# A decoder layer on one core: order of the first loads, order of the products in a chunk, transposes of the identity at the start, rotation tables earlier

## Chip, cores and metric

The kernel runs on one core of one Trainium2 chip. The metric is device time in microseconds (us) of one execution. The median of three runs is given, and one more execution was profiled.

## The reference, cut to what matters

One layer for 256 tokens of 2048 features, in float32: a gated feed-forward half (FFN), a mixer of retention and sliding-window attention side by side, a second FFN half, and a gated embedding, each followed by a layer norm. What the change touches is the first FFN and the cosine and sine tables of the rotary positions.

```python
def swiglu(x, w_gu, w_down):
    g, u = jnp.split(x @ w_gu, 2, axis=-1)
    return (jax.nn.silu(g) * u) @ w_down
...
def rotary(x, pos, n_rot, theta):
    half = n_rot // 2
    inv = 1.0 / (theta ** (jnp.arange(half, dtype=jnp.float32) / half))
    ang = pos.astype(jnp.float32)[..., None] * inv
    cos = jnp.cos(ang)[:, :, None, :]
    sin = jnp.sin(ang)[:, :, None, :]
...
h = layer_norm(alpha * h + 0.5 * swiglu(h, w_ffn1_gu[i], w_ffn1_down[i]), ln_g[i, 0], ln_b[i, 0])
```

## The kernel before

**Products.** A float32 product is made of three passes over a high and a low part of each operand. `split` (L91, L92) makes the parts: ScalarE casts the high part, then VectorE subtracts it to get the low part. `Sum.add` issues the three matmuls of 128x512 (L298: low left part by high right part, L299: high by high, L300: high by low). The weights come as chunks of 512 KB: `Chunk` loads one (L105), and `make` splits it. In the trace a gate or up chunk is rf_gu when raw, and hf_gu and lf_gu are its parts. A chunk holds two tiles of 128 features (k tiles). The 256 tokens are two halves t = 0 and 1, each with a PSUM bank of its own. `tokens_chunk` walks over halves and k tiles, so a chunk that serves both halves is 12 matmuls.

**Blocks.** The gate and up products of the first FFN go in 11 blocks (`ffn`, `block`), tiles f1g and f1u. Block 0 has eight ordinary units, each a gate chunk and an up chunk over the same two k tiles: 16 chunks. Later blocks have ordinary units and some of seven products (`Seven`): VectorE forms the sums u and v of a pair of chunks (L163 to L166), and these and the raw chunks are split (huf_gu, luf_gu, hvf_gu, lvf_gu, bf_gu among the results). Their extra sums go to the banks f11s in block 1 and f12s in block 2. They need sums of the inputs, which `seven_forms` makes ahead of unit 7 of block 0 (tiles sums, f1fh, f1fl). At the end of block 0, ScalarE applies Silu to the gate banks (L833) and VectorE multiplies by the up banks (L835), giving f1v. Two takes of chunks later, `turned` transposes the result on TensorE against the identity (f1t, L774), and ScalarE copies it out of its banks (f1a, L776).

**Order of the work.** Each engine runs its instructions in the order in which the program wrote them (`manual_schedule`). `plan` is the list of weight units in their order of use. `fill` is called after each unit and writes two kinds of work. It writes the split of the next loaded unit while the units that are ready are worth under 45 matmuls and while the slots allow it. It writes loads of further units, if after the load there is still room to split the unit in front. `slots_for_weights` sets how many slots weights may use, 6 at the start and 24 from unit 6 of block 0. A raw ordinary chunk needs one slot and a split one keeps two. So 6 slots hold the splits one chunk ahead of the products. Slots are counted as the program is written, not as it runs. Loads go on SyncE's DMA queue, the first chunk and the constants on that of ScalarE. A transfer's completion semaphore is one of eight in turn, so a queue waits until the transfer eight places earlier in the program has landed.

**The start.** `first_chunk` and `load_x_chunk` bring in x, transposed, in four parts (xraw, split into xt). A part has four k tiles, and the first one comes as four pieces of 128 KB. The first weight chunk comes as two halves on ScalarE's queue. ident, the identity for transposes, is written by GpSimd at the start. At unit 2 of block 0 `load_constants` issues four small transfers on ScalarE's queue, and `rotary_tables` is appended to `lazy`. It is a generator. Each `next` writes one step: the load of the positions; their cast (L689) with six operations on the angle (L696 to L701); pairs of L704; a last L704; a clamp (L708); a sine on ScalarE (L710); five operations (L712 to L716); a cosine (L718). The steps from the angle on come twice, for retention (rotr) and for attention (rota). `run_side`, called after each chunk, runs one such step.

Of the kernel before, what the change touches and what calls it, by code (L numbers as in the profile page):

```python
# [15 lines left out]
P = 128  # L16
S = 256
# [11 lines left out]

HELD_MIX = 4  # L30
FRONT = 6
FRONT_PAIRS = 3
HELD_PAIRS = 2, 3
SLOTS = 46
# [14 lines left out]
def layer(ctx: ExitStack, tc: tile.TileContext, io):  # L49
    nc = tc.nc  # L50
    sync, act, dve, pool, pe = nc.sync, nc.scalar, nc.vector, nc.gpsimd, nc.tensor
# [8 lines left out]
    def bank(name):  # L60
        return psum.tile([P, 512], F32, tag="ps", name=name)
# [12 lines left out]
    plan = []  # L74
# [15 lines left out]
    def split(dst_hi, dst_lo, src, lo_engine=None):  # L90
        act.copy(dst_hi, src)  # L91
        (lo_engine or dve).tensor_tensor(dst_lo, src, dst_hi, ALU.subtract)  # L92
# [88 lines left out]
    loaded, ready = [], []  # L181
    room = {"slots": 0, "used": 0, "ahead": 45, "far": 90, "quiet": False}
# [41 lines left out]
    def slots_for_weights(n, ahead=45, far=90):  # L224
        room.update(slots=n, ahead=ahead, far=far)
# [5 lines left out]
    lazy = []  # L231
# [71 lines left out]
        return tuple(x[:, t * P : (t + 1) * P] for x in a)  # L303

    def tokens_chunk(chunk, k0, lhs, sums, ts, kks=(0, 1)):
        for t in ts:
            for kk in kks:
                sums[t].add(half_of(lhs(k0 + kk), t), chunk.columns(kk))

    def tokens_out(key, n_k, lhs, ps, n=512, before=None):  # L310
# [352 lines left out]
    ident = const.tile([P, P], F32, name="ident")  # L663
# [7 lines left out]
    ht = big.tile([P, KD, 512], F32R, tag="ht", name="xt")  # L671
# [12 lines left out]
    def rotary_tables():  # L684
        pos_i = slot([P, S], I32, "pos_i")
        act.dma_start(pos_i, io["positions"].broadcast_to([P, S]))
        pos = slot([P, S], F32, "pos")
        yield
        dve.tensor_copy(pos, pos_i)  # L689
        table = slot([P, 4, S], F32, "trig")  # L690
        trig.extend(table[:, j, :] for j in range(4))
        cos_r, sin_r, cos_a, sin_a = trig
        for inv, sgn, cos, sin, nm in ((0, 2, cos_r, sin_r, "r"), (1, 3, cos_a, sin_a, "a")):
            w = slot([P, 4, S], F32, "rot" + nm)
            ang, n, na, nb = (w[:, j, :] for j in range(4))
            dve.tensor_scalar(ang, pos, cst[:, inv : inv + 1], None, ALU.mult)  # L696
            dve.tensor_scalar(n, ang, INV_2PI, MAGIC, ALU.mult, ALU.add)
            dve.tensor_scalar(n, n, MAGIC, None, ALU.subtract)
            dve.tensor_scalar(na, n, 1.0 / 2048.0, MAGIC, ALU.mult, ALU.add)
            dve.tensor_scalar(na, na, MAGIC, 2048.0, ALU.subtract, ALU.mult)  # L700
            dve.tensor_tensor(nb, n, na, ALU.subtract)  # L701
            yield
            for who, j in ((na, 0), (nb, 0), (na, 1), (nb, 1), (na, 2), (nb, 2), (na, 3)):
                dve.scalar_tensor_tensor(ang, who, -TWO_PI[j], ang, ALU.mult, ALU.add)  # L704
                if who is nb:
                    yield
            yield
            dve.tensor_scalar(n, ang, 3.1415925, -3.1415925, ALU.min, ALU.max)  # L708
            yield
            act.activation(nb, n, AF.Sin)  # L710
            yield
            dve.tensor_scalar(sin, nb, cst[:, sgn : sgn + 1], None, ALU.mult)  # L712
            dve.tensor_scalar(na, ang, 1.5707963267948966, None, ALU.add)
            dve.tensor_scalar(n, na, 3.141592653589793, -6.283185307179586, ALU.is_gt, ALU.mult)
            dve.tensor_tensor(na, na, n, ALU.add)
            dve.tensor_scalar(na, na, 3.1415925, -3.1415925, ALU.min, ALU.max)  # L716
            yield
            act.activation(cos, na, AF.Sin)  # L718
            yield
# [35 lines left out]

    def ffn(name, i, ht, norm, keep, residual, keepers, away):
        if i == 0:
            slots_for_weights(6)
        rhs = lambda k: (ht[:, k, :S], ht[:, k, S:])
        raws = []  # L760
        made = {}
# [23 lines left out]
        for j in range(KF // 4):  # L785
            pg, pu = banks(f"{name}g{j}"), banks(f"{name}u{j}")
            units = gu_units(j)
            plain = len(units) - sum(kind == "S" for kind, p in units)
            n_of = {(0, 0): KD, (0, 1): KD, (1, 0): KD, (1, 1): KD}
            for kind, p in units:  # L790
                if kind == "S":
                    for at in ((0, 0), (0, 1), (1, 0)):
                        n_of[at] -= 1
                    n_of[1, 1] -= 2
            sums = [[Sum((pg, pu)[n][t], n_of[t, n]) for n in range(2)] for t in range(2)]
            got = []

            if norm is not None and j == 0:
                front, units = units[:FRONT_PAIRS], units[FRONT_PAIRS:]
                steps = [(gu_keys(name, 0)(n, p), 2 * p, n) for _, p in front for n in range(2)]  # L800
                norm.first(steps, rhs, sums, (
                    (3, (1, 0)), (5, (1, 1)), (7, (0, 2)), (8, (1, 2)), (9, (0, 3)), (10, (1, 3)), (10, "go"),
                ))
                slots_for_weights(24)

            def before(u, j=j, offset=KD // 2 - len(units)):
                u += offset
                if j == 0 and norm is None and u % 2 == 0:
                    first_chunk(u // 2)
                    if u == 6:  # L810
                        slots_for_weights(24)
                    if u == 2:
                        load_constants()
                        lazy.append(rotary_tables())
                if j == 0 and u == 7:
                    for g in sorted({p // 2 for p in SEVEN}):
                        hi, lo = (slot([P, 8, P], F32R, f"{name}f{w}{g}") for w in "hl")
                        made[g] = seven_forms(keep[g], hi, lo)
                if j == KF // 4 - 1 and u in (4, 6):
                    convert(u // 2 - 2)  # L820

            block(f"{name}{j}", units, gu_keys(name, j), rhs, forms, sums, lambda *a: got.extend(seven_common(*a)), before)
            if got:
                g, v = got
                for x, ps in ((g, pg), (v, pu)):
                    for t in range(2):
                        dve.tensor_tensor(x[:, t], x[:, t], ps[t], ALU.add)  # L827
                act.activation(g, g, AF.Silu)  # L828
                dve.tensor_tensor(v, g, v, ALU.mult)
            else:  # L830
                v = slot([P, 2, 512], F32, f"{name}v{j}")
                for t in range(2):
                    act.activation(v[:, t], pg[t], AF.Silu)  # L833
                for t in range(2):
                    dve.tensor_tensor(v[:, t], v[:, t], pu[t], ALU.mult)  # L835
            later(2, lambda j=j, v=v: turned(j, v))
# [558 lines left out]
    x_parts = {}  # L1395

    def load_x_chunk(c):
        raw = slot([P, 4, S], F32, f"xraw{c}")
        x_parts[c] = raw
        pieces = 4 if c == 0 else 1  # L1400
        parts = [slice(j * 4 // pieces, (j + 1) * 4 // pieces) for j in range(pieces)]
        for at in parts:
            sync.dma_start(raw[:, at], io["xT"][c][:, at])
        if c == 0:
            u = plan.pop(0)
            u.load(pieces=2, queue=act)
            u.chunk.make_hi()
            room["used"] += u.keeps
            ready.append(u)
        for j, at in enumerate(parts):  # L1410
            to = ht[:, 4 * c : 4 * c + 4, :][:, at]
            split(to[:, :, :S], to[:, :, S:], raw[:, at])
            if c == 0 and j < 2:
                u.chunk.make_part(u.chunk.parts[j])

    with tc.manual_schedule():
        warm = small.tile([P, 1], F32, tag="nc1", name="warm")
        dve.memset(warm, 0.0)
        act.activation(warm, warm, AF.Silu)
        plan_ffn("f1")  # L1420
        plan.extend(Single(("w_pp", blk, 0)) for blk in range(2))
        plan_mixers()
        plan.extend(Single(("w_pp", blk, 0)) for blk in range(2, 4))
        plan_ffn("f2")
        for blk in range(4):
            plan_tokens(("w_pg", blk), KD)
        kept = sorted({p // 2 for p in SEVEN})
        norm = ffn("f1", 0, ht, None, x_parts, x_columns, (), rows[0])
        norm = mixers(norm.new, norm, rows[0], kept, rows[1])
        norm = ffn("f2", 2, norm.new, norm, norm.keep, rows[1], (), None)  # L1430
        embedding(norm.new, norm, norm.y)
        assert not (plan or loaded or ready or side or lazy) and not room["used"]
# [100 lines left out]
```

## Time and profile before

| | |
|---|---|
| three runs | 2291.86, 2292.39, 2293.10 us |
| profiled execution | 2292.7 us, span 2290.8 us |
| mean granted TensorE clock | 0.998 |
| TensorE busy | 2266.2 us |
| VectorE busy | 1945.5 us |
| ScalarE busy | 1183.6 us |
| HBM read, written | 455.43 MB, 8.39 MB |

In the profile PE is TensorE, PEld its loading of stationary operands, DVE VectorE, ACT ScalarE, POOL GpSimd and SP SyncE. A q behind a name means the queue or sequencer of that engine. The timeline gives start, duration, engine, line, operation and tiles (out<-in). In brackets stands the idle time of the engine before the instruction, with what ended it. In the list of waits a line gives who waited for whom, then the total in us, how many times, and the longest. In the windows each engine has its busy time and in brackets its number of instructions, in the order PE, PEld, DVE, ACT, POOL, followed by the clock, the DMA share and GB/s. All times are from the start of the span.

### The profile page before, as it was taken

Reading aid. Unit: us, or ns where it says so; the run is one execution under the profiler, and the core shown is the slowest. Engines: PE = TensorE matmul, PEld = TensorE weight load, DVE = VectorE, ACT = ScalarE, POOL = GpSimd, SP = SyncE. Lnnn points to the kernel's source line nnn. Section 1 sums busy time; section 2 is a strip of 40 time slices with the busy share of each in tenths; the row PEclk is TensorE's granted clock in tenths of the full one; section 3 lists DMA queues with packets and bytes.
Section 4 is the critical chain, followed back from the end, with each engine's and each line's share of the span. In section 5 each row is a group of like instructions: output and inputs, shape, how many; then the busy total and the mean of one; then the engine's idle time right before and its main releaser. Section 6 shows DMA issues by size and latency. Waiting matters only on the chain.

```text
span 2290.8 us, 28764 instructions
## 1 busy us (share of the span) xinstructions
PE 2266.2 (99%) x10466; PEld 1879.6 (82%) x10466; DVE 1945.5 (85%) x2467; ACT 1183.6 (52%) x1427; POOL 95.8 (4%) x53
## 2 busy tenths in 40 slices
PE   9999999999999999999999999999999999999997
PEld 7788888888888888888778888888888888888876
DVE  7999999998989774677789786779999999889876
ACT  5555555555554342435556454355565555555532
POOL 0000000000000530124000000000000000000000
PEclk9999999999999999999999999999999999999999
DMA  9576666665587565555447567576656566565771
GB/s 317 167 220 193 185 210 197 190 203 191 209 287 275 181 227 163 171 165 158 138 156 238 168 223 276 186 234 208 194 190 211 183 199 216 182 221 193 276 275 55
DMA packets 193725, 465.70 MB, mean 203 GB/s; under 512 B 14768, under 2 KB 16048, under 8 KB 193584
## 3 DMA queue, kind: packets, MB, share of 16 engines
q1 hardware_dynamic: 191456, 460.91, 60.9%
q10 hardware_dynamic: 2128, 2.97, 0.4%
q8 instruction: 82, 1.34, 0.2%
q14 instruction: 59, 0.48, 0.1%
HBM read 455.43 MB, written 8.39 MB: 202 GB/s over the span
## 4 chain that ended last, share of the span: by engine, by line
PE 96%; DVE 3%; DMA 1%; issue 0%; ACT 0%; SPq 0%; ACTq 0%; DVEq 0%
PE f1g L298 3%; PE f1g L299 3%; PE f1g L300 3%; PE f2g L298 3%; PE f2g L300 3%; PE f2g L299 3%; PE rqk L249 3%; PE f1u L299 2%; PE f1u L300 2%; PE f1u L298 2%; PE f2u L298 2%; PE f2u L299 2%; PE f2u L300 2%; PE aqk L249 2%; PE f1d L300 2%; PE f2d L299 2%
## 5 line engine op out<-in xcount | busy, mean ns | idle before, releaser
L92 DVE TENSOR_TENSOR lf_gu<-rf_gu,hf_gu 128x1024 fp32r<-128x1024 f32 (+1 forms) x283 | 334.5, 1215 | 10.2 <-ACT hf_gu L91 9.8
L91 ACT CAST hf_gu<-rf_gu 128x1024 fp32r<-128x1024 f32 (+1 forms) x283 | 281.9, 1046 | 18.5 <-DMA rf_gu<-in_f_gu 18.5
L92 DVE TENSOR_TENSOR lw_in_f<-rw_in_f,hw_in_f 128x1024 fp32r<-128x1024 f32 x140 | 195.7, 1428 | 29.2 <-ACT hw_in_f L91 26.6
L92 DVE TENSOR_TENSOR lf_down<-rf_down,hf_down 128x1024 fp32r<-128x1024 f32 x152 | 181.0, 1221 | 27.9 <-ACT hf_down L91 23.5
L91 ACT CAST hf_down<-rf_down 128x1024 fp32r<-128x1024 f32 x152 | 155.2, 1050 | 76.0 <-DMA rf_down<-in_f_down 26.4
L91 ACT CAST huf_gu<-uf_gu 128x1024 fp32r<-128x1024 f32 x70 | 73.7, 1054 | 159.4 <-DVE uf_gu L164 156.8
L91 ACT CAST hw_in_f<-rw_in_f 128x1024 fp32r<-128x1024 f32 x140 | 138.9, 1051 | 2.4 <-DMA rw_in_f<-in_w_in_f 2.1
L298 PE MATMUL f1g<-hf_gu,xt 128*128 128x512 f32 x247 | 97.2, 393 | 5.4 <-ACT hf_gu L91 5.4
L299 PE MATMUL f1g<-hf_gu,xt 128*128 128x512 f32 x247 | 96.8, 392 | 0.0
L300 PE MATMUL f1g<-lf_gu,xt 128*128 128x512 f32 x247 | 96.8, 392 | 0.0
L298 PE MATMUL f2g<-hf_gu,ht 128*128 128x512 f32 x247 | 96.3, 390 | 0.0
L300 PE MATMUL f2g<-lf_gu,ht 128*128 128x512 f32 x247 | 96.2, 389 | 0.0
L299 PE MATMUL f2g<-hf_gu,ht 128*128 128x512 f32 x247 | 96.1, 389 | 0.0
L91 ACT CAST hvf_gu<-vf_gu 128x1024 fp32r<-128x1024 f32 x70 | 73.8, 1054 | 29.5 <-DVE vf_gu L166 28.9
L828 ACT ACTIVATE eve<-eve 128x1024 f32<-128x1024 f32 x20 | 21.2, 1062 | 127.0 <-DVE eve L827 127.0
L92 DVE TENSOR_TENSOR luf_gu<-uf_gu,huf_gu 128x1024 fp32r<-128x1024 f32 x70 | 85.3, 1219 | 0.0
L92 DVE TENSOR_TENSOR lvf_gu<-vf_gu,hvf_gu 128x1024 fp32r<-128x1024 f32 x70 | 85.3, 1218 | 0.0
L298 PE MATMUL f2u<-hf_gu,ht 128*128 128x512 f32 x212 | 83.7, 395 | 0.0
L298 PE MATMUL f1u<-hf_gu,xt 128*128 128x512 f32 x212 | 83.4, 393 | 0.0
L300 PE MATMUL f2u<-lf_gu,ht 128*128 128x512 f32 x212 | 82.6, 390 | 0.0
L299 PE MATMUL f2u<-hf_gu,ht 128*128 128x512 f32 x212 | 82.6, 389 | 0.0
L299 PE MATMUL f1u<-hf_gu,xt 128*128 128x512 f32 x212 | 82.5, 389 | 0.0
(1333 smaller groups left out, 6425.9 us busy)
## 6 DMA issues: line engine op xcount, KB each, us to landing
rf_gu<-in_f_gu SPq DMA_DIRECT2D x351, 512.0 KB, 4.9
rf_down<-in_f_down SPq DMA_DIRECT2D x176, 512.0 KB, 4.5
rw_in_f<-in_w_in_f SPq DMA_DIRECT2D x148, 512.0 KB, 4.3
rw_rv<-in_w_rv SPq DMA_DIRECT2D x32, 512.0 KB, 4.7
rw_ret<-in_w_ret SPq DMA_DIRECT2D x32, 512.0 KB, 4.5
rw_mix<-in_w_mix SPq DMA_DIRECT2D x32, 512.0 KB, 3.9
rw_pg<-in_w_pg SPq DMA_DIRECT2D x32, 512.0 KB, 5.2
rw_att<-in_w_att SPq DMA_DIRECT2D x16, 512.0 KB, 4.9
```

Source lines behind the costliest of these rows:

```text
L91: act.copy(dst_hi, src)
L92: (lo_engine or dve).tensor_tensor(dst_lo, src, dst_hi, ALU.subtract)
L249: pe.matmul(ps[f], hi[:, kk, f * P : (f + 1) * P], rhs(k), start=k == 0, stop=k == n_k - 1,)
L298: pe.matmul(o, al, bh, start=first, stop=False)
L299: pe.matmul(o, ah, bh, start=False, stop=False)
L300: pe.matmul(o, ah, bl, start=False, stop=self.left == 0)
L828: act.activation(g, g, AF.Silu)
```

## The change

The first part of x comes as three pieces (one k tile, one k tile, two k tiles). The second weight chunk is loaded ahead of the third piece. Nine slots instead of six are open to weights until unit 6 of block 0. `tokens_chunk` takes k tile by k tile, both halves of the tokens for each, instead of half by half. Fourteen transposes of the identity stand on TensorE ahead of the first product. The generator of the rotation tables gets one more step ahead of each of the units 4 to 7 of block 0.

```diff
@@ -29,6 +29,8 @@
 
 HELD_MIX = 4
 FRONT = 6
+
+WARM = 14
 FRONT_PAIRS = 3
 HELD_PAIRS = 2, 3
 SLOTS = 46
@@ -303,8 +305,8 @@
         return tuple(x[:, t * P : (t + 1) * P] for x in a)
 
     def tokens_chunk(chunk, k0, lhs, sums, ts, kks=(0, 1)):
-        for t in ts:
-            for kk in kks:
+        for kk in kks:
+            for t in ts:
                 sums[t].add(half_of(lhs(k0 + kk), t), chunk.columns(kk))
 
     def tokens_out(key, n_k, lhs, ps, n=512, before=None):
@@ -755,7 +757,7 @@
 
     def ffn(name, i, ht, norm, keep, residual, keepers, away):
         if i == 0:
-            slots_for_weights(6)
+            slots_for_weights(9)
         rhs = lambda k: (ht[:, k, :S], ht[:, k, S:])
         raws = []
         made = {}
@@ -812,6 +814,8 @@
                     if u == 2:
                         load_constants()
                         lazy.append(rotary_tables())
+                if j == 0 and u >= 4 and lazy and next(lazy[0], "end") == "end":
+                    lazy.pop(0)
                 if j == 0 and u == 7:
                     for g in sorted({p // 2 for p in SEVEN}):
                         hi, lo = (slot([P, 8, P], F32R, f"{name}f{w}{g}") for w in "hl")
@@ -1397,21 +1401,36 @@
     def load_x_chunk(c):
         raw = slot([P, 4, S], F32, f"xraw{c}")
         x_parts[c] = raw
-        pieces = 4 if c == 0 else 1
-        parts = [slice(j * 4 // pieces, (j + 1) * 4 // pieces) for j in range(pieces)]
-        for at in parts:
+        if c:
+            sync.dma_start(raw, io["xT"][c])
+            split_x(c, slice(0, 4))
+            return
+        parts = [slice(0, 1), slice(1, 2), slice(2, 4)]
+        for at in parts[:2]:
             sync.dma_start(raw[:, at], io["xT"][c][:, at])
-        if c == 0:
-            u = plan.pop(0)
-            u.load(pieces=2, queue=act)
-            u.chunk.make_hi()
-            room["used"] += u.keeps
-            ready.append(u)
+        u = plan.pop(0)
+        u.load(pieces=2, queue=act)
+        u.chunk.make_hi()
+        room["used"] += u.keeps
+        ready.append(u)
+        plan[0].load()
+        room["used"] += plan[0].loads
+        loaded.append(plan.pop(0))
+        sync.dma_start(raw[:, parts[2]], io["xT"][c][:, parts[2]])
         for j, at in enumerate(parts):
-            to = ht[:, 4 * c : 4 * c + 4, :][:, at]
-            split(to[:, :, :S], to[:, :, S:], raw[:, at])
-            if c == 0 and j < 2:
+            split_x(c, at)
+            if j < 2:
                 u.chunk.make_part(u.chunk.parts[j])
+
+    def split_x(c, at):
+        to = ht[:, 4 * c : 4 * c + 4, :][:, at]
+        split(to[:, :, :S], to[:, :, S:], x_parts[c][:, at])
+
+    def warm_up():
+
+        ps = bank("warm")
+        for _ in range(WARM):
+            pe.transpose(ps[:, :P], ident, ident)
 
     with tc.manual_schedule():
         warm = small.tile([P, 1], F32, tag="nc1", name="warm")
@@ -1425,6 +1444,7 @@
         for blk in range(4):
             plan_tokens(("w_pg", blk), KD)
         kept = sorted({p // 2 for p in SEVEN})
+        warm_up()
         norm = ffn("f1", 0, ht, None, x_parts, x_columns, (), rows[0])
         norm = mixers(norm.new, norm, rows[0], kept, rows[1])
         norm = ffn("f2", 2, norm.new, norm, norm.keep, rows[1], (), None)
```

## The prediction

> **What bounds the kernel now.** I read the page first, then TensorE's waits in the first 130 us, then the timelines of TensorE, ScalarE, VectorE and the DMA queue there, because the change acts there and nowhere else by design. TensorE's waits after 113 us were listed too: 3.3 us in all, every one at a norm.
>
> ```profile
> PE 2266.2 (99%) x10466; PEld 1879.6 (82%) x10466; DVE 1945.5 (85%) x2467; ACT 1183.6 (52%) x1427; POOL 95.8 (4%) x53
> PE 96%; DVE 3%; DMA 1%; issue 0%; ACT 0%; SPq 0%; ACTq 0%; DVEq 0%
> ```
>
> TensorE is busy for 99% of the span and carries 96% of the chain that ended last. The change takes no product away, so it can only win back waits or slow matmuls. The waits of the first 130 us:
>
> ```profile
> PE f1g L298 <- ACT hf_gu L91: 5.4, 2, 5.2
> PE f12s L298 <- ACT f1a L776: 1.0, 1, 1.0
> PE f11s L300 <- DVE luf_gu L92: 0.6, 1, 0.6
> PE f11s L300 <- DVE lvf_gu L92: 0.2, 1, 0.2
> ```
>
> 5.2 us pass before the first product, 0.2 us at the second half chunk, and 1.8 us in blocks 1 and 2. Slow matmuls show in TensorE's timeline:
>
> ```profile
> 8.94 0.63 PE L299 MATMUL f1g<-hf_gu,xt 128*128 128x512 f32 x1
> 9.37 0.57 PE L300 MATMUL f1g<-lf_gu,xt 128*128 128x512 f32 x1
> 9.78 0.39 PE L298 MATMUL f1g<-hf_gu,xt 128*128 128x512 f32 x1
> 10.01 0.40 PE L299 MATMUL f1g<-hf_gu,xt 128*128 128x512 f32 x1
> ```
>
> Starts are 0.43 us apart until 9.8 us and 0.227 us apart after it (0.227 is the median from 10 us on). All that is slow is some ten matmuls: 10 x 0.20 = 2.0 us. Now the supply of the first two chunks and of the positions, on ScalarE and VectorE:
>
> ```profile
> 6.39 0.62 ACT L91 CAST hf_gu<-rf_gu 128x512 fp32r<-128x512 f32 x1 [0.90 <-DMA rf_gu<-in_f_gu]
> 8.47 1.04 ACT L91 CAST hf_gu<-rf_gu 128x1024 fp32r<-128x1024 f32 x1 [0.84 <-DMA rf_gu<-in_f_gu]
> 9.55 1.23 DVE L92 TENSOR_TENSOR lf_gu<-rf_gu,hf_gu 128x1024 fp32r<-128x1024 f32 x1 [1.14 <-ACT hf_gu L91]
> 24.16 0.29 DVE L689 CAST pos<-pos_i 128x256 f32<-128x256 int32 x1 [1.44 <-DMA pos_i<-in_positions]
> 36.39 0.42 ACT L710 ACTIVATE rotr<-rotr 128x256 f32<-128x256 f32 x1 [2.63 <-DVE rotr L708]
> 37.78 3.50 DVE L92 TENSOR_TENSOR lf_gu<-rf_gu,hf_gu 128x1024 fp32r<-128x1024 f32 x3 [0.29 <-ACT hf_gu L91]
> 56.78 1.28 DVE L835 TENSOR_TENSOR f1v<-f1v,f1u 128x512 f32<-128x512 f32 x2
> 57.00:80.00 23.00, 23.00 (x107) 19.13 (x106) 22.59 (x34) 12.02 (x16) 0.00 (x0) 1.00 0.62 188
> 80.00:110.00 30.00, 28.97 (x130) 23.10 (x128) 29.55 (x36) 16.87 (x20) 0.00 (x0) 1.00 0.50 160
> ```
>
> The last two lines are the windows: VectorE (third pair) is busy 22.59 of 23 and 29.55 of 30 us. From the landing of the positions at 24.16 us to 113 us it runs back to back; its few pauses are 0.3 us at 37.78 and 1.2 us in each of the two `seven_forms`. So **VectorE, not TensorE, sets when blocks 1 and 2 pass**: TensorE catches it up at 85.4 us (0.6 and 0.2 us) and at 110 us. There TensorE waits for f1a, ScalarE's copy of a bank, which stands behind casts (hvf_gu at 109.17) that waited for VectorE's v sums. After 113 us TensorE waits for nothing in the blocks, so what it is late then, it is late at the end.
>
> **The change part by part** (c0 to c15 are the 16 chunks of block 0, gate and up in turn).
>
> *Identity transposes.* 14, of the kind of f1t (8 in 0.87 us of the chain, 0.11 each): 1.5 us at that pitch, double at the slow one, so from ident's end (1.3 us) to 2.8 or 4.1 us. The first product still waits for c0's first half at 5.24 us. They delay nothing; they may speed up the ten slow matmuls, at most 2.0 us.
>
> *Order of the products.* In every chunk with both token halves, feature tile 0 now serves both halves before tile 1. Tile 0 of c0 gives 6 matmuls instead of 3 before c0's second half is needed at 7.06: at full clock they end at 5.24 + 6 x 0.227 = 6.6, then the other six run to 8.4 (before: 10.24). Changes of bank cost nothing in the trace: over the whole run the pitch from L300 to L298 is 0.227 us (median) with a change of bank and without. One bank of a block ends three matmuls (0.7 us) later, the last one at the same time, so its reader finishes no later. The second half's features are wanted 0.7 us earlier behind a norm; at the gate stage they are written at 2204.5 and wanted at 2206.3 then. Both zero.
>
> *Loads.* SyncE now issues x0a, x0b (the first two k tiles of x), c1, x0cd (the other two of the first four), c2, c3, x1. With x0 and c0 the bytes up to the last of c1 and x0cd are as before, so the later of the two, now x0cd, lands where c1 did, 8.4. ScalarE's queue has x0cd's cast ahead of c1's: 8.4 + 0.6, then c1's cast 9.0 to 10.05, VectorE's low part to 11.25 (before: 10.78). c1's third matmul needs that low part. So c1 ends at 11.25 + 10 x 0.227 = 13.5 against 13.23. **The ten slow matmuls are won and handed back to c1**; it is the same with a slow clock, as c0 then ends at 10.3, still ahead of 11.25. TensorE alone: +0.3 us.
>
> *Nine slots instead of six.* `fill` needs two free slots to make a chunk; used slots stop at 8 instead of 4, so VectorE's queue runs three chunks ahead of the products instead of one. The transfers in these 25 us follow each other without a gap (a chunk lands each 1.35 us), so chunks do not come sooner; x1, x2, the constants and the positions stand two chunks later in their queues. x2 was cast at 16.59; now about 16.59 + 2 x 1.35 = 19.3. The constants' issues on ScalarE's queue follow it; positions were issued 1.95 us after it (18.54), now 21.25, and land 5.6 us later: 26.85. VectorE has by then made two chunks more, to 24.6 us, and waits 2.25 us instead of 1.44. At 29.2 us it has c1 to c9, the positions' cast and six steps of the table; before it had at 29.2 us 0.4 us less of c9 and two L704 steps (0.8 us) more: it is 0.4 us later. Bounds: no wait at all gives -1.85; a landing after 7.5 us, as the chunks' median in the first 30 us, gives +2.3. I take 5.6, this transfer's own row; its neighbours took 4.9 to 6.0.
>
> *Rotation steps.* An extra `next` ahead of units 4 to 7. The work is the same, its place is not. Now the clamp (L708) is directly followed by the sine, and c14's cast stands behind the sine on ScalarE, with no low part in between on VectorE. From the clamp's end (36.36) to the end of the cast behind the sine (37.77) are 1.4 us, of which 0.3 were idle before: +1.1 us. The second table's sine stands behind block 1's first seven-product chunk, whose low parts cover it: 0.
>
> Of the second table five L704 steps and a clamp (2.4 us) now come before f1v at 56.78. f1v ends 2.4 + 0.4 + 1.1 = 3.9 us later, at 62.0; TensorE's f1t wanted it at 59.5 (+0.3). TensorE loses some 2.2 us there and some 0.7 at the next ordinary chunk, and finds the waits of 0.8 and 1.0 us at 85 and 110 us gone in exchange; it meets VectorE again at 110 us. There only VectorE's lateness counts, since its work to that point is the same.
>
> Sum: 0.4 + 1.1 = **+1.5 us** at 110 us, kept to the end. The profiled execution took 2292.7 us (span 2290.8 and 1.9 around), so 2294.2 by its own time; it lies 0.3 above the median of 2292.39, hence 2293.9 for the median.
>
> [...]
>
> **The rivals.** About 0.2% (4.6 us) is what a measurement of this kernel can tell from no change, and the first two rivals stay inside it.
>
> 1. *The fast start is kept.* If x0cd lands with c1 and VectorE's wait for the positions shrinks by 2 us, the 2.0 us of slow matmuls reach the end: 2290.4. For it: TensorE has no other wait until 59 us. Against it: c1's low part and a VectorE that is full to 113 us. Chance 0.2. Even with all waits of 85 and 110 us (1.8) gone too it is 3.8, under 0.2%; over that it needs something unseen: 0.03.
> 2. *Nothing moves.* Transposes that leave the clock as it is, positions that land 1.5 us sooner: 2292.4. Part of the forecast's own spread.
> 3. *Slower for good: the positions land late.* Everything on VectorE stands behind that cast. From 26.85 us on, each us of their landing is a us at the end. Two chunks more are in the queue; transfers with eight in flight took 7.5 us at the median, and if this one took 10, the end is 1.5 + 4.4 = 5.9 us later: 2298.3. It decides from 8.7 us after the issue (1.5 + 3.1 = 4.6). Against it: the four neighbours at 4.9 to 6.0. Chance 0.1.
>
> **How the numbers follow.** VectorE decides (-0.7 to +3.4 us, from the bounds of the landing): 0.67, time 2293.9. Rival 1: 0.23, of it 0.03 beyond 0.2%. Rival 3: 0.1. The range reaches from rival 1 with 0.5 us of the waits at 85 and 110 us on top to the forecast's upper bound: 2289.9 to 2295.8. Faster 0.03, within 0.2% 0.87, slower 0.10.
>
> **What would show it.** Right: 14 transposes ahead of 5 us; c1's third matmul near 11.3 us behind its low part; a pause of VectorE near 2 us ahead of the positions' cast at 26 to 27 us; about 1.4 us idle between the clamp and the next low part; TensorE waiting 1 to 2 us at f1t near 60 us; waits at 85 us gone; block 2 passing 110 us about 1 us later. Wrong: c1 done well before 13.2 us with block 2 earlier as well, or new waits of TensorE after 113 us.

## The result, and the profile after

| | before | after |
|---|---|---|
| median of 20 runs each | 2292.45 us | 2295.64 us |
| lowest and highest | 2291.30, 2293.63 | 2294.28, 2298.02 |
| profiled execution, span | 2292.7, 2290.8 us | 2295.68, 2293.7 us |

The changed kernel takes 1.0014 times as long as before (95% interval 1.0008 to 1.0021). The ratio is inside the bound of 0.2%, though the interval excludes equal times and its upper end is just past that bound. The forecast was 2293.9 us, 1.7 below the median.

In the profile after, the helpers stand two lines lower (L92 is now L94, L298 to L300 are L300 to L302, L774 is L776, L835 is L839). Busy times and the chain, from the page:

```profile
PE 2268.9 (99%) x10480; PEld 1880.8 (82%) x10480; DVE 1945.3 (85%) x2466; ACT 1183.6 (52%) x1426; POOL 95.5 (4%) x53
PE 93%; DVE 4%; DMA 2%; issue 1%; ACT 0%; SPq 0%; ACTq 0%; DVEq 0%
```

VectorE and ScalarE do what they did. TensorE has 14 instructions more, the transposes. In the chain VectorE, DMA and issue each take 1% more of the span, and TensorE 3% less. TensorE's waits in the first 130 us:

```profile
PE f1g L300 <- ACT hf_gu L93: 1.9, 2, 1.0
PE warm L1433 <- POOL ident masks.py:199: 1.4, 1, 1.4
PE f1g L302 <- DVE lf_gu L94: 1.2, 2, 0.7
PE f12s L300 <- ACT f1a L778: 1.0, 1, 1.0
PE f1u L300 <- ACT hf_gu L93: 0.6, 1, 0.6
PE f1u L302 <- DVE lf_gu L94: 0.5, 1, 0.5
PE f1t L776 <- DVE f1v L839: 0.2, 1, 0.2
```

The waits for luf_gu and lvf_gu at 85 us (0.8) are gone and others have come for hf_gu and lf_gu. TensorE's timeline shows where these lie:

```profile
1.36 3.11 PE L1433 MATMUL warm<-ident 128*128 128x128 f32 x14 [1.36 <-POOL ident masks.py:199]
5.49 0.50 PE L300 MATMUL f1g<-hf_gu,xt 128*128 128x512 f32 x1 [1.02 <-ACT hf_gu L93]
10.81 0.50 PE L302 MATMUL f1u<-lf_gu,xt 128*128 128x512 f32 x1 [0.53 <-DVE lf_gu L94]
57.80 0.50 PE L300 MATMUL f1g<-hf_gu,xt 128*128 128x512 f32 x1 [0.90 <-ACT hf_gu L93]
59.24 0.50 PE L302 MATMUL f1g<-lf_gu,xt 128*128 128x512 f32 x1 [0.71 <-DVE lf_gu L94]
62.12 0.98 PE L776 MATMUL f1t<-ident,f1v 128*128 128x128 f32 x7 [0.19 <-DVE f1v L839]
71.50 0.50 PE L302 MATMUL f1g<-lf_gu,xt 128*128 128x512 f32 x1 [0.45 <-DVE lf_gu L94]
```

The transposes end at 4.47 us. c0 then runs at full pitch, c1 waits for its low part at 10.81, and the third chunk starts at 13.21, 0.02 us from where it started before. So the full clock of the start brought nothing. The time that TensorE lost lies at 57.8 and 59.2 us (1.6), 62.1 (0.2) and 71.5 us (0.45). VectorE and ScalarE in the same profile:

```profile
27.07 0.29 DVE L691 CAST pos<-pos_i 128x256 f32<-128x256 int32 x1 [3.11 <-DMA pos_i<-in_positions]
38.16 0.42 ACT L712 ACTIVATE rotr<-rotr 128x256 f32<-128x256 f32 x1 [4.20 <-DVE rotr L710]
39.55 1.23 DVE L94 TENSOR_TENSOR lf_gu<-rf_gu,hf_gu 128x1024 fp32r<-128x1024 f32 x1 [1.43 <-ACT hf_gu L93]
60.78 1.28 DVE L839 TENSOR_TENSOR f1v<-f1v,f1u 128x512 f32<-128x512 f32 x2
71.73 1.23 DVE L94 TENSOR_TENSOR lf_gu<-rf_gu,hf_gu 128x1024 fp32r<-128x1024 f32 x1 [0.29 <-ACT hf_gu L93]
86.27 1.22 DVE L94 TENSOR_TENSOR luf_gu<-uf_gu,huf_gu 128x1024 fp32r<-128x1024 f32 x1
57.00:80.00 23.00, 20.85 (x92) 16.50 (x93) 22.47 (x31) 16.70 (x22) 0.00 (x0) 1.00 0.59 184
80.00:110.00 30.00, 30.00 (x137) 24.66 (x136) 29.52 (x36) 14.62 (x18) 0.00 (x0) 1.00 0.59 192
```

VectorE waits 3.11 us for the positions (issued at 20.52 by ScalarE's queue), 1.43 us behind the clamp and 0.29 us behind the second table's cosine. It is full again from 57 to 110 us, while TensorE is now the one that idles, 2.15 us of 23 in the first window. The last luf_gu of block 1 is a mark that every version has, behind all of the moved steps. Before it was

```profile
84.14 1.22 DVE L92 TENSOR_TENSOR luf_gu<-uf_gu,huf_gu 128x1024 fp32r<-128x1024 f32 x1
```

and after it starts at 86.27: **VectorE is 2.13 us late.** TensorE's wait at f12s stands at 112.9 instead of 110.75, and the last f1t transposes of the half start at 485.41 instead of 483.32: 2.1 us late for good. Behind the first norm it is 2.4 (first rqk product at 741.47 for 739.09) and behind the third one 2.95 (first product of w_pg at 2187.95 for 2185.0), against 2.98 for the whole execution.

### The profile page after: what moved, and what is told of

The parts are those of the page before. It is cut to its first block, busy times and chain, and to the rows that moved or that the text cites. A ratio compares the mean times of both kernels' runs of the same rounds, so it can differ in the third digit from the quotient of the medians.

```text
span 2293.7 us, 28797 instructions
## 1 busy us (share of the span) xinstructions
PE 2268.9 (99%) x10480; PEld 1880.8 (82%) x10480; DVE 1945.3 (85%) x2466; ACT 1183.6 (52%) x1426; POOL 95.5 (4%) x53
## 4 chain that ended last, share of the span: by engine, by line
PE 93%; DVE 4%; DMA 2%; issue 1%; ACT 0%; SPq 0%; ACTq 0%; DVEq 0%
PE f2g L302 3%; PE f2g L301 3%; PE f2g L300 3%; PE rqk L251 3%; PE f2u L301 2%; PE f2u L300 2%; PE f2u L302 2%; PE f1g L302 2%; PE f1g L300 2%; PE f1g L301 2%; PE f1u L302 2%; PE f1u L301 2%; PE f1u L300 2%; PE aqk L251 2%; PE f2d L302 2%; PE f1d L302 2%
## 5 line engine op out<-in xcount | busy, mean ns | idle before, releaser
L94 DVE TENSOR_TENSOR lf_gu<-rf_gu,hf_gu 128x1024 fp32r<-128x1024 f32 (+1 forms) x283 | 334.2, 1214 | 10.1 <-ACT hf_gu L93 9.6
L94 DVE TENSOR_TENSOR lw_in_f<-rw_in_f,hw_in_f 128x1024 fp32r<-128x1024 f32 x140 | 195.6, 1427 | 29.4 <-ACT hw_in_f L93 26.8
L94 DVE TENSOR_TENSOR lf_down<-rf_down,hf_down 128x1024 fp32r<-128x1024 f32 x152 | 180.9, 1220 | 25.9 <-ACT hf_down L93 21.0
L300 PE MATMUL f1g<-hf_gu,xt 128*128 128x512 f32 x247 | 96.4, 390 | 1.9 <-ACT hf_gu L93 1.9
L302 PE MATMUL f1g<-lf_gu,xt 128*128 128x512 f32 x247 | 96.6, 391 | 1.2 <-DVE lf_gu L94 1.2
L300 PE MATMUL f2g<-hf_gu,ht 128*128 128x512 f32 x247 | 96.3, 390 | 0.0
L302 PE MATMUL f2g<-lf_gu,ht 128*128 128x512 f32 x247 | 96.2, 390 | 0.0
L94 DVE TENSOR_TENSOR luf_gu<-uf_gu,huf_gu 128x1024 fp32r<-128x1024 f32 x70 | 85.3, 1218 | 0.0
L94 DVE TENSOR_TENSOR lvf_gu<-vf_gu,hvf_gu 128x1024 fp32r<-128x1024 f32 x70 | 85.3, 1218 | 0.0
L300 PE MATMUL f1u<-hf_gu,xt 128*128 128x512 f32 x212 | 83.5, 394 | 0.6 <-ACT hf_gu L93 0.6
L300 PE MATMUL f2u<-hf_gu,ht 128*128 128x512 f32 x212 | 83.8, 395 | 0.0
L302 PE MATMUL f1u<-lf_gu,xt 128*128 128x512 f32 x212 | 82.7, 390 | 0.5 <-DVE lf_gu L94 0.5
L302 PE MATMUL f2u<-lf_gu,ht 128*128 128x512 f32 x212 | 82.6, 390 | 0.0
```

Source lines behind the costliest of these rows:

```text
L300: pe.matmul(o, al, bh, start=first, stop=False)
L302: pe.matmul(o, ah, bl, start=False, stop=self.left == 0)
```

## Experiments

**The theory:** VectorE's lateness at that mark reaches the end. It has three terms, the positions' landing, the pause behind the clamp and the pause behind the second cosine. TensorE's own start counts for nothing. **Rivals:** (a) the start on TensorE, transposes or order of products, costs the time; (b) the nine slots cost it, by other slots and so other waits hundreds of microseconds later, above all at the third norm.

All times are medians of 11 runs, against 15 to 33 runs of the kernel before on the same chip. "Mark" is the shift of the last luf_gu of block 1 in the version's profile against 84.14.

| version | difference of medians, us | ratio, 95% interval | mark, us |
|---|---|---|---|
| order_only | 0.0 | 1.0001 [0.9992, 1.0010] | +0.1 |
| nine_slots_only | +0.4 | 1.0002 [0.9993, 1.0010] | +0.4 |
| steps_between_chunks | +0.5 | 1.0002 [0.9993, 1.0011] | +0.6 |
| no_steps | +1.1 | 1.0005 [0.9996, 1.0014] | +0.9 |
| steps_only | +1.4 | 1.0007 [0.9998, 1.0016] | +1.0 |
| after_no_identity | +1.5 | 1.0008 [0.9999, 1.0017] | +1.5 |
| after_early_positions | +1.5 | 1.0008 [0.9999, 1.0017] | +0.9 |
| six_slots | +1.9 | 1.0008 [0.9999, 1.0017] | +1.8 |
| the change | +3.2 | 1.0014 [1.0008, 1.0021] | +2.1 |
| after_sine_apart | +4.7 | 1.0022 [1.0013, 1.0030] | +3.5 |
| before_early_positions | -0.6 | 0.9996 [0.9987, 1.0005] | -1.7 |
| start_and_early_constants | -1.4 | 0.9994 [0.9984, 1.0003] | -2.6 |
| before_early_constants | -1.9 | 0.9992 [0.9983, 1.0001] | -2.2 |

Of the twelve only after_sine_apart has an interval that excludes 1. No part is therefore shown by its time alone. What carries the reading is that medians and marks rise together over 14 kernels; none of them moves by more than 1.3 us against its mark. A mark is read from one execution. In the five profiles that issue the positions at 20.5 to 20.8 us these took 5.8 to 6.7 us to land, so a mark can move by some 0.5 us (an estimate from that spread) by this alone.

### The steps alone

```diff
+                if j == 0 and u >= 4 and lazy and next(lazy[0], "end") == "end":
+                    lazy.pop(0)
```

These two lines were added to the kernel before.

> The kernel before with the extra rotation step ahead of units 4 to 7 of block 0 alone. Theory (VectorE's ledger: each us that VectorE stands idle before block 2 is a us at the end): the sine behind the clamp holds up VectorE by 1.43 us instead of 0.29, and the pause of 0.29 us at 71.7 us after the change comes with it, so +1.1 to +1.4 us, 2293.6 to 2293.9; the positions land at 24.1 us as before and cost nothing more. Rival 1 (the start or the order of products costs it): within 0.3 us of before. Rival 2 (the late f1v, not VectorE's total, sets the end): +2 us or more, with no wait of TensorE left at block 2's f12s.

Measured: 2293.64 us, +1.4. VectorE's timeline of this kernel:

```profile
36.16 1.23 DVE L92 TENSOR_TENSOR lf_gu<-rf_gu,hf_gu 128x1024 fp32r<-128x1024 f32 x1 [1.43 <-ACT hf_gu L91]
```

The pause behind the clamp is there with nothing else of the change, at the same 1.43 us: 1.14 more than the 0.29 before. The positions' cast, at 23.68, was 0.5 earlier in this profile, and the mark is at 85.12, +0.98.

### The order of the products alone

```diff
-        for t in ts:
-            for kk in kks:
+        for kk in kks:
+            for t in ts:
```

> The kernel before with tokens_chunk walking k tile by k tile alone. Theory: within 0.4 us of before (2292.1 to 2292.9), as a change of PSUM bank costs nothing and the last bank of a block ends when it did. Rival (the 0.8 us that the change loses at the norms, behind 600 us, come from the bank that ends three matmuls later): +0.5 to +1.0 us, with the new wait of 0.2 us at the first norm's transposes and 0.5 us at the third norm's.

Measured: 2292.27 against 2292.28 us, mark +0.1. The order costs and brings nothing in the median, so this half of rival (a) is out, within the interval. Its profile does hold the new wait at the first norm's transposes which the rival named, and which the kernel before does not have there:

```profile
707.28 0.44 PE L516 MATMUL lnps<-ident,f1y 128*128 128x128 f32 x2 [0.35 <-DVE f1y L509]
```

The first rqk product begins 0.5 us later than before in this profile, and at the third norm 0.3 us are won back.

### The change without the steps

```diff
-                if j == 0 and u >= 4 and lazy and next(lazy[0], "end") == "end":
-                    lazy.pop(0)
```

> The changed kernel without the extra rotation step: loads, order, slots and identity transposes stay. Theory: VectorE waits for the positions some 3.1 us and is 0.65 us later than before by work done; no pause at the sine. +0.7 us at block 2, and up to 0.8 more if the loss at the norms does not belong to the rotation steps: 2293.1 to 2293.9. Rival (the steps cost nothing, the start costs it all): 2295.2 or more.

Measured: 2293.33 us, +1.1, mark +0.9. What is left is the landing:

```profile
27.33 0.29 DVE L691 CAST pos<-pos_i 128x256 f32<-128x256 int32 x1 [3.33 <-DMA pos_i<-in_positions]
```

A wait of 3.33 us instead of 1.44, part of it made good by the chunks that VectorE had already split. The two halves, 0.98 by the steps and 0.85 by the loads and slots, make 1.83 of the 2.13.

### The change with six slots, and nine slots alone

```diff
# six_slots, in the changed kernel
-            slots_for_weights(9)
+            slots_for_weights(6)
# nine_slots_only, in the kernel before
-            slots_for_weights(6)
+            slots_for_weights(9)
```

> The changed kernel with six slots for weights in block 0 instead of nine. x2, the constants and the positions come two chunks earlier in their queues again. Theory: positions land near 24 us, VectorE's wait for them falls to about 1.5 us, and it is 0.6 to 0.8 us earlier than in the changed kernel: 2294.8 to 2295.0. Rival (chunks made three ahead of the products are worth something, so six slots lose it): 2295.9 or more.

> The kernel before with nine slots for weights in block 0 instead of six, nothing else. Theory, first part: x2, the constants and the positions stand two chunks later, VectorE waits about 3 us for the positions and is 0.6 to 0.9 us late at block 2. Second part (new): the slots are handed out in another order from then on, so that two loads of the gate stage near 2170 us wait for VectorE's fold (f2y) and the third norm loses 0.5 us. Both: 2293.2 to 2293.7. Rival (slots given out early cost nothing at the end): 2292.9 at most, and the gate stage's loads as before.

Measured: six_slots 2294.21 us, +1.9, mark +1.8; nine_slots_only 2293.07 against 2292.69 us, +0.4, mark +0.4. The first is 0.6 us below what was expected, the second 0.1 us below its theory and 0.2 us above its rival. The positions' cast with six slots starts at 24.53, behind a wait of 1.98 us; with nine slots alone it is in VectorE's timeline:

```profile
26.83 0.29 DVE L689 CAST pos<-pos_i 128x256 f32<-128x256 int32 x1 [2.65 <-DMA pos_i<-in_positions]
```

Nine slots do move the cast back, by 2.67 us (26.85 was forecast), but VectorE has more chunks split by then, so the mark shows only 0.4. With six slots the landing is nearly that of before, and the mark's 1.8 is mostly the steps' pauses. The third norm of nine_slots_only passed as before (31.7 us from the last product into f2d1s, the extra sums of the second FFN half's down product, to the first product of w_pg, against 31.6), so nine slots alone did not make the 0.55 us there: rival (b) fails in this simple form.

### The transposes taken away

```diff
-        warm_up()
```

> The changed kernel without the fourteen transposes of the identity. Theory: the slow clock comes back for the first ten or so matmuls, c0 ends near 10.3 us and c1 still waits for its low part at 10.8 to 11.3, so the time is within 0.4 us of the changed kernel's 2295.6. Rival (the transposes win 2 us which the rest of the change loses): 2297.2 or more.

Measured: 2294.21 against 2292.69 us, +1.5, mark +1.5, 1.0 us below the expected range. The third chunk begins at 13.37 instead of 13.21. No gain of the transposes shows: without them the difference to before is +1.5 instead of +3.2. In the profiles 0.6 us of that lies at the mark, where the positions' cast came at 26.45 instead of 27.07, and 0.6 in the third norm, which took 31.6 us instead of 32.2. The intervals of the two ratios overlap, so that the transposes cost time is not shown.

### The sine kept apart from the clamp

```diff
-                if j == 0 and u >= 4 and lazy and next(lazy[0], "end") == "end":
+                if j == 0 and u in (4, 6, 7) and lazy and next(lazy[0], "end") == "end":
```

Without the extra step of unit 5, a chunk stands between the first clamp and its sine again.

> The changed kernel with the extra rotation step ahead of units 4, 6 and 7 only, so that the clamp and the sine have a chunk between them again. Theory: VectorE's pause there falls from 1.43 to 0.3 us, 2294.3 to 2294.7. Rival (what costs is that five steps and the clamp come ahead of f1v): 2295.3 or more, as only one step less comes ahead of it.

Measured: 2297.35 us, +4.7, mark +3.5: the slowest of all, and 2.7 us above the expected range. The pause behind the clamp fell to 0.29 us, but every later pair shifted by one, and two others now stand back to back. VectorE's timeline:

```profile
43.60 1.23 DVE L94 TENSOR_TENSOR lf_gu<-rf_gu,hf_gu 128x1024 fp32r<-128x1024 f32 x1 [1.49 <-ACT hf_gu L93]
70.34 1.23 DVE L94 TENSOR_TENSOR lf_gu<-rf_gu,hf_gu 128x1024 fp32r<-128x1024 f32 x1 [1.42 <-ACT hf_gu L93]
```

In the first the cast stood behind the cosine of table 1, in the second behind the sine of table 2. That the second table's sine finds cover, as the prediction had it, no longer holds here. The second pause also holds up f1a, ScalarE's copy. TensorE's timeline:

```profile
70.84 0.70 PE L300 MATMUL f11s<-huf_gu,f1fl 128*128 128x512 f32 x1 [2.27 <-ACT f1a L778]
71.34 0.63 PE L301 MATMUL f11s<-huf_gu,f1fh 128*128 128x512 f32 x1
74.60 0.39 PE L300 MATMUL f1g<-hf_gu,xt 128*128 128x512 f32 x1
```

A wait of 2.27 us was followed by 0.43 us per matmul until 74.4. One pause was taken away and the time rose: it is the place that the program gives to each dependent pair that decides, as a term of 1.1 to 1.5 us each.

### The positions earlier

```diff
+    def load_positions():
+        pos_i = slot([P, S], I32, "pos_i")
+        sync.dma_start(pos_i, io["positions"].broadcast_to([P, S]))
+        positions.append(pos_i)
 ...
     def rotary_tables():
-        pos_i = slot([P, S], I32, "pos_i")
-        act.dma_start(pos_i, io["positions"].broadcast_to([P, S]))
+        pos_i = positions.pop()
 ...
         if c < 3:
             load_x_chunk(c + 1)
+        if c == 0:
+            load_positions()
```

The load of the positions leaves the first step of `rotary_tables` and stands on SyncE's queue behind the second part of x (x1); once in the kernel before, once in the changed one.

> The kernel before with the positions loaded on SyncE's queue right behind x1, so that they land near 11 us; all steps of the tables stay where they are. Theory (VectorE's ledger): its 1.44 us wait for the positions goes, blocks 1 and 2 pass 1.2 to 1.4 us earlier as TensorE's waits of 0.8 and 1.0 us there shrink: 2290.9 to 2291.1. Rival (TensorE or the transfers bound the first 110 us): within 0.4 us of before, with the waits of TensorE at 85 and 110 us unchanged.

> The changed kernel with the positions loaded on SyncE's queue right behind x1; steps, order, slots and transposes stay. Theory (VectorE's ledger): its wait of 3.1 us for the positions goes, of which 2 us or so are kept (a chunk that lands near 27 us takes the rest), block 2 passes 2 us earlier: 2293.0 to 2294.0. Rival (what the change loses lies in the rotation steps and behind 600 us, not at the positions): 2295 or more.

Measured: before_early_positions 2292.05 against 2292.69 us, -0.6, mark -1.7, and no wait of TensorE at 85 or 110 us. The mark moved by 0.3 us more than the theory says, but only some four tenths of it show in the median, so the expectation of 2290.9 to 2291.1 was missed by 1 us; the profiled execution, 2290.21, was the fastest of its runs. after_early_positions: 2293.92 against 2292.38 us, +1.5, mark +0.9. Here the cast stands at 25.78 without a wait. The positions' term is gone and the mark fell from +2.1 to +0.9, which is about what the steps alone cost.

### The constants earlier too

```diff
+        sync.dma_start(pos_i, io["positions"].broadcast_to([P, S]))
+        sync.dma_start(cst, io["cst"])
 ...
     def load_constants():
-        act.dma_start(cst, io["cst"])
 ...
-                        load_constants()
+                if j == 3 and u == 0 and norm is None:
+                    load_constants()
```

In the kernel before, the small table cst follows the positions on SyncE's queue, and the three other small transfers (mask, gn and sink, which only the mixers read) are issued ahead of block 3. start_and_early_constants is the changed kernel with that, six slots and no extra steps, and with c1 split ahead of the third piece of x:

```diff
         for j, at in enumerate(parts):
+            if j == 2:
+                make_next()
             split_x(c, at)
```

> The kernel before with the positions and the small table of constants loaded on SyncE's queue right behind x1, and the mask and the two other small transfers issued ahead of block 3 instead of in block 0. Theory: VectorE's 1.44 us wait goes, and no load waits for the small transfers any more (SyncE's queue stood 3.3 us behind one of them), so that VectorE is 1.4 to 2.2 us earlier at block 2; TensorE, which then never waits from 14 us to the first norm, sets the end: 2290.6 to 2291.8. Rival (block 3 pays for the four transfers): within 0.4 us of before.

> The version that the runs point to: the kernel before_early_constants with the changed kernel's identity transposes, order of products and order of loads, but six slots, no extra rotation steps, and the second chunk split ahead of the third piece of x. Theory: VectorE is early enough at block 2 that the start of TensorE counts at last; c1's low part is ready near 9.5 us instead of 10.8 and c0 runs at the full clock, 1.0 to 1.7 us on top: 2289.2 to 2290.6. Rival (VectorE still sets blocks 1 and 2): no better than before_early_constants, with waits of TensorE at 85 or 110 us.

Measured: before_early_constants 2290.49 against 2292.38 us, -1.9, mark -2.2. In its first 130 us TensorE waits 5.3 us for the first product and 0.4 us for one low part. The windows:

```profile
57.00:80.00 23.00, 23.00 (x107) 19.15 (x106) 22.52 (x34) 13.80 (x17) 0.00 (x0) 1.00 0.58 197
80.00:110.00 30.00, 30.00 (x138) 24.88 (x137) 29.62 (x36) 17.45 (x21) 0.00 (x0) 1.00 0.52 165
```

TensorE is busy in all of both windows: the 1.8 us that the kernel before lost in blocks 1 and 2 are won, about the difference of the medians. This is the lowest median of the case, though its interval still reaches 1. Which of the moved transfers brings what beyond before_early_positions was not run apart. start_and_early_constants: 2291.03 us, -1.4, mark -2.6. The start of the change added to it brought nothing, against an expectation of 2289.2 to 2290.6: VectorE is 0.4 us earlier still, but TensorE no longer waits for it. In its profile the first products ran at half rate until 10.2 us in spite of the transposes, and the third chunk began at 13.07.

### The steps kept between chunks

```diff
+    free = [True]
 ...
+            free[0] = False      # behind a table's clamp
+            free[0] = True       # behind its cosine
 ...
+                if j == 0 and u >= 4 and lazy and free[0] and next(lazy[0], "end") == "end":
+                    lazy.pop(0)
```

The kernel before with the extra steps, but none of them between a table's clamp and its cosine.

> The kernel before with the extra rotation step ahead of units 4 to 7, but not from the clamp of a table to its cosine, so that every sine and cosine keeps a chunk ahead of it; two steps more than before fit into block 0. Theory (an activation of ScalarE right behind its VectorE step is what costs): all pauses of VectorE at the tables stay at 0.3 us, the time is within 0.4 us of before, some 1 us under steps_only. Rival (table steps ahead of f1v cost, wherever the sine stands): +1 us or more.

Measured: 2293.09 against 2292.59 us, +0.5, mark +0.6. VectorE's timeline:

```profile
36.87 1.23 DVE L92 TENSOR_TENSOR lf_gu<-rf_gu,hf_gu 128x1024 fp32r<-128x1024 f32 x1 [0.29 <-ACT hf_gu L91]
```

The pause is 0.29 us as before, and the version is 0.9 us lower than steps_only against its reference; 0.5 us is just over the 0.4 that was expected. The positions' cast began 0.5 us earlier than before in the profile of steps_only and 0.2 us later in this one, so from the cast on the steps cost VectorE some 1.5 us there and 0.4 here. By these two profiles the pauses, not the tables' earlier place, are most of what the steps cost; the intervals of the two ratios overlap.

## Why the prediction was right, and by how much its steps were off

The time lay inside the range and on the side of no difference, by the mechanism that was forecast: VectorE's lateness at block 2 reaches the end. The size was off by a factor of two, and the median lies only 0.16 us under the top of the range, 2295.8: that the range held is in part luck. By the profiled executions the sum should have been +1.5 us and was +2.98:

| step | forecast | measured |
|---|---|---|
| positions' late landing | +0.4 | +0.7 |
| pause from clamp to sine | +1.1 | +1.14 |
| second table | 0 | +0.3 |
| order of products | 0 | 0 (order_only) |
| norms | 0 | +0.85 |
| sum | +1.5 | +2.99 |

- **Positions: the term was too small.** They were issued at 20.52, not 21.25, and landed 6.5 us later rather than 5.6; the cast started at 27.07 for 26.85. VectorE had made its chunks by 23.96 instead of 24.6, so the wait was 3.1 for 2.25 us. The 0.7 is what is left of the mark's 2.13 when the other two pauses are taken off. Counted by work done it comes out alike: the cast is 2.91 us later than before, but two more chunks of 1.13 us each are split by then, so VectorE is 0.65 us late.
- **Clamp to sine: right**, to 0.04 us and at its place; steps_only has it alone and steps_between_chunks takes it away.
- **Second table: mis-sized.** The sine was covered by the seven-product chunk, as forecast. The cosine was not costed: the low part behind it at 71.73 waited 0.29 us.
- **The start: right.** The full clock was won in this profile (full from 4.20 us; that the transposes bring it was an estimate, which three of the six profiles with them bear out) and handed back to c1, which waited for its low part at 10.81 (forecast 11.25) and ended at 13.2 (13.5). The transposes ended at 4.47 us; the 4.1 of the prediction is a slip, as 1.3 us and twice 1.5 make 4.3. The rival of the kept fast start is refuted: its 2.0 us did not reach the end here.
- **f1v: its end was right, the place of the loss was not.** f1v ended at 62.06, forecast 62.0. TensorE was to lose 2.2 us at f1t and 0.7 behind it. It lost 0.9 and 0.7 at the third chunk of block 1, at 57.8 and 59.2 us, since that chunk's split stands in the same late queue ahead of f1v; 0.2 at f1t and 0.45 at 71.5. The waits at 85 us are gone as forecast, the one at f12s stayed at 1.0 us.
- **Norms: the step that failed.** "After 113 us TensorE waits for nothing in the blocks, so what it is late then, it is late at the end" holds up to the norms, where 0.85 us were added; the term had been put at nothing. New waits of TensorE after 113 us were named as a sign of being wrong, and two came. TensorE's waits at the norm's transposes, first two lines before, last two after:

```profile
PE lnps L516 <- DVE f1y L509: 1.0, 2, 0.5
PE lnps L516 <- DVE f2y L509: 0.7, 2, 0.4
PE lnps L518 <- DVE f1y L511: 1.2, 3, 0.5
PE lnps L518 <- DVE f2y L511: 1.2, 3, 0.5
```

At the first norm (f1y) TensorE's lateness grew from 2.1 to 2.4 us; at the third (f2y) from 2.4 to 2.95. The new wait at the first norm, 0.21 us at 709.17, is of the kind that order_only has too, so the order of the products may be part of it: the profiles with the old order have at most 0.1 us there, four of the eight with the new order 0.2 to 0.4 us. The waits for the stretch from 2160 us, where the loads and splits of w_pg stand, the first two lines after, the last one before:

```profile
SPq L107 <- DVE f2y L861: 1.7, 2, 1.3
DVE lw_pg L94 <- ACT hw_pg L93: 2.1, 2, 1.1
DVE lw_pg L92 <- ACT hw_pg L91: 1.4, 2, 0.7
```

The first line is SyncE's queue, from 2160 to 2180 us, the other two are VectorE's, from 2160 to 2190. SyncE's loads waited for slots that VectorE's fold f2y frees, and a low part of w_pg waited 1.1 us for its cast. In after_no_identity SyncE waits there 0.4 us for ncur and 0.3 us for evw instead.

The long passage of the third norm (32.2 to 32.4 us instead of 31.6) is in the profiles of the change, no_steps and after_sine_apart. It is not in nine_slots_only, six_slots (which has a wait of 1.4 us on f2y too) or after_no_identity. So among these it goes with nine slots and the transposes together; but after_early_positions has both and took 31.9 us, and the profiles without the two together range from 30.9 (steps_only) to 31.7. Why is **not settled**: that the two change which tile gets which slot is an argument, not a measurement. Nor can 0.55 us of one execution be told from scatter, since the runs of one kernel lie 1.4 to 4.6 us apart.

Of the rivals, the late landing of the positions went part of the way: 6.5 us after the issue, where it decides from 8.7.

## What to carry to other kernels

When two in-order engines feed the bound one, add up the idle time of the feeder, not that of the bound engine: here, as far as the profiles tell, every 0.3 to 1.5 us that VectorE lost ahead of 85 us came out at the end while it was the late one, and 2 us of full clock at the start came to nothing. Once TensorE no longer waited for it, time won on VectorE was no longer won at the end (mark -2.6 against -1.4 us in start_and_early_constants). A step on one engine and the step on another that reads it should have other work written between them on both (VectorE's pause behind the clamp was 1.43 us without it in steps_only, 0.29 with it in steps_between_chunks); where a moved step is placed, check each such pair that shifts with it. A small transfer that is issued late can hold up a full engine that waits for it (VectorE waited 3.11 us for the positions in the change): loading the positions early is what all three versions with a lower median have in common (down to -1.9 us in before_early_constants, with other small transfers moved too; the three intervals still reach 1).

## What the runs showed of the hardware

- **Work ahead of the first product gave the full clock early in only some executions.** With the same 14 transposes from 1.36 to about 4.5 us, the granted clock became full at 4.20, 4.71 and 4.10 us in the profiles of the change, no_steps and six_slots, and only at 9.52, 14.06 and 10.18 in after_sine_apart, after_early_positions and start_and_early_constants. In eight profiles without them it was 8.4 to 11.6 us. Why the same transposes gave it at 4.10 us once and at 14.06 us once is not shown: in after_early_positions TensorE worked from 1.36 us on and paused for no more than 0.69 us.
- **The full clock was lost again behind waits in two profiles.** In six_slots it fell at 10.92 us, after waits of 1.13 and 0.53 us, and came back at 14.34; TensorE's timeline there:

```profile
10.76 0.67 PE L302 MATMUL f1u<-lf_gu,xt 128*128 128x512 f32 x1 [0.53 <-DVE lf_gu L94]
14.51 0.39 PE L302 MATMUL f1u<-lf_gu,xt 128*128 128x512 f32 x1
```

In after_sine_apart it fell at 70.96, after the wait of 2.27 us, and came back at 74.38. In the change's profile, with waits of 0.56 and 0.53 us for the second chunk at 9.55 and 10.81 us, it stayed full. How much idle time it takes is not settled by these three cases.
